# A decoder layer on one core: GpSimd sums the squares of two norms, the last output tile is multiplied ahead of its norm, and one gate operand is split in two parts

## The chip, the cores and the metric

The kernel runs on one core of one Trainium2 chip. The metric is the device time of one execution in microseconds (us), as the median of several runs. The engines are called PE (TensorE, the matrix unit), DVE (VectorE), ACT (ScalarE), POOL (GpSimd) and SP (SyncE, which here only issues transfers).

## The reference

One layer of a hybrid decoder with 1024 tokens, model width 1024 and an FFN width of 2816, all in float32. Two groups of heads (a gated delta rule and a differential attention) give `o_la` and `o_d`; what follows them is what the change touches:

```python
def rmsnorm(x, w, eps=1e-6):
    return x * lax.rsqrt(jnp.mean(x * x, axis=-1, keepdims=True) + eps) * w
...
x = x + concatenate([o_la, o_d]) @ w_out
h = rmsnorm(x, ffn_norm_w)
gate, up = split(h @ w_gate_up, 2)
x = x + (silu(gate) * up) @ w_down
return rmsnorm(x, final_norm_w)
```

## The kernel before

**Tiles and stages.** The 1024 rows are eight row tiles t = 0 to 7 of 128 rows; a row tile's 1024 columns are worked on in two halves of 512. Each float32 operand of a product is kept as two rounded parts, h (a cast on ACT) and l (a subtraction of h from the value), and a product is three matmuls, h·h, l·h and h·l. The helper `parts` (L1153) writes both: its cast runs on ACT, its subtraction on the engine given. A subtraction that helper `parts` makes bears line L1155, the cast L1154. After the attention part come four stages: the output product with the FFN norm and the transposes (about 605 to 683 us), the first block of the gate and up products, f = 0 (to 707), the loop over the remaining 21 blocks (to 1090), the down product (to 1293), and the final norm with the output (to the end at 1325.5).

**The FFN norm.** `unit_d` (L1189) runs the last matmuls of the output product for one half of one row tile; an addition on DVE (L828) puts them on the residual. Then `half_h` (L1134) squares the half on ACT with the sum of its columns as a by-product (L1140, followed by a read of the accumulator). After the second half of a tile DVE adds the two sums (L1144) and forms mean + 1e-6 (L1145), POOL raises it to the power -1/2 (L1147), and DVE multiplies both halves by this factor and the norm's weights in two `scalar_tensor_tensor` instructions (L1149). The row tiles come in the order 4, 5, 6, 7, 0, 1, 2, 3.

**The transposes.** `trans_h` (L1162) transposes a normed row tile in eight matmuls (L1166). Gate and up are computed in seven half-size products per block (Strassen's scheme in Winograd's form), so the transposed activations are quarters and sums of quarters: B11 (lower half of the width) and B21 (upper half) from the row tiles 0 to 3, B12 and B22 from 4 to 7, and T1 to T4 as sums. They carry the names hB1 (B11 and B21 together), hB22 and hT1 to hT4, with `_h` and `_l` for the parts. For t below 4 both halves of hB1 are cast in one ACT instruction 1024 wide (L1180) and subtracted in one DVE instruction 1024 wide (L1183).

**The first block.** PE runs the seven products of f = 0 in the order S3·T3, S4·B22, A11·B11, S1·T1, S2·T2, A12·B21, A22·T4 (L1381 to L1414), twelve matmuls each (L1250), and the transposes of the last row tile, `trans_h(3)`, stand between the first two in the code. The weights' sums S1 to S4 are made on DVE (L1218, L1365, L1366) and split by `parts`; `late_operands` makes those of A11, S1, S2, A12 and A22. The weights of the next block are fetched by `w_prepare`, into two buffers for the gate columns and one for the up columns, so the next up weights can only be fetched when A22 has been split.

**The end.** `final_sum` (L1566) adds the last matmuls to the residual on DVE (L1262) and squares them on ACT (L1572); `final_norm` (L1574) adds the two sums and forms the mean on DVE (L1576, L1577) and the power on POOL (L1579); `final_out` (L1582) makes the first half with a scaled copy on ACT (L1587) and a multiplication by the weights `wb3` on POOL (L1588), and the second half with one `scalar_tensor_tensor` on DVE (L1590). For the last row tile, t = 7, both halves are made on DVE. Each half is written by SP (L1592).

**What sets the order.** A scheduler orders the instructions of PE, ACT, POOL and SP, and of DVE too up to the last loop; only in the last loop (L1594 to L1603) DVE follows the order of the code:

```python
for t in range(NT):
    if t + 1 < NT: final_sum(t + 1, 0)
    ssn = final_norm(t)
    if t + 1 < NT: final_sum(t + 1, 1)
    final_out(t, ssn)
```

Each engine runs its own instructions strictly in order and waits for others by semaphores.

## Time and profile before

| | |
|---|---|
| median of 3 runs (lowest to highest) | 1322.28 us (1320.35 to 1322.42) |
| profiled execution, own time | 1327.25 us |
| profiled execution, span from first to last instruction | 1325.5 us |
| mean granted TensorE clock | 0.986 of full speed |
| PE busy | 1268.9 us, 96% of the span |
| DVE busy | 836.6 us, 63% |
| ACT busy | 537.1 us, 41% |
| POOL busy | 299.4 us, 23% |

The profiled execution is one execution; its span leaves out what lies before the first and after the last instruction, and its own time (1.75 us longer) is the figure that the runs' times compare with. Busy time of an engine says how long its instructions ran, not whether another engine waited for them; that is read from the timeline of an engine, where the idle time before an instruction stands in brackets with what ended it.

### The profile page before, as it was taken

How to read it: one execution, taken by the hardware profiler on the slowest of the kernel's cores; microseconds unless marked ns; L12 is line 12 of the kernel's file. 1: busy time of each engine (PE TensorE's matmuls, PEld its weight loads, DVE VectorE, ACT ScalarE, POOL GpSimd, SP SyncE). 2: the span in 40 equal slices, each digit the busy share in tenths (PEclk: the TensorE clock that was granted, in tenths of full speed). 3: DMA queues.
4: the chain of work that ended last, by engine and by line, in shares of the span. 5: the costliest groups of instructions: out<-in, count | busy, mean ns of one | idle time of the engine just before them, and what ended most of it. 6: DMA issues, size and time to landing. Idle time of an engine off the chain costs nothing.

```text
span 1325.5 us, 17315 instructions
## 1 busy us (share of the span) xinstructions
PE 1268.9 (96%) x6432; PEld 1064.5 (80%) x6432; DVE 836.6 (63%) x1380; ACT 537.1 (41%) x1038; POOL 299.4 (23%) x235
## 2 busy tenths in 40 slices
PE   6999989999999988999989999999999999999996
PEld 6978878898988776877768888888888888778775
DVE  6515758724766566865886655566566536687877
ACT  5324432222657555543552333333333317243314
POOL 1014443200022433023322212222212110121104
PEclk9999999989999998999989999999999999999999
DMA  7426664301053654744513343233323346666503
GB/s 222 116 64 206 219 211 136 119 17 32 17 163 118 183 192 167 208 166 176 171 47 112 112 134 108 91 119 120 112 99 108 104 159 239 206 238 207 178 13 127
DMA packets 143883, 183.43 MB, mean 138 GB/s; under 512 B 15888, under 2 KB 92984, under 8 KB 143800
## 3 DMA queue, kind: packets, MB, share of 16 engines
q1 hardware_dynamic: 135888, 168.19, 39.7%
q10 hardware_dynamic: 7912, 14.16, 2.9%
q8 instruction: 50, 0.82, 0.3%
q14 instruction: 33, 0.27, 0.1%
HBM read 127.00 MB, written 55.32 MB: 138 GB/s over the span
## 4 chain that ended last, share of the span: by engine, by line
PE 43%; DVE 5%; issue 1%; ACT 1%; DMA 1%; POOL 1%; POOLq 0%; DVEq 0%; ACTq 0%
PE big L1250 17%; PE sm L1250 8%; PE big L1549 5%; PE fl L1250 4%; PE fl L1549 3%; PE sm L1549 3%; DVE ebl L1265 1%; DMA w_raw<-in_w_gate_up 1%; DVE xh L1218 1%; PE fl L148 0%; PE fl L150 0%; PE fl L149 0%; DVE x L1262 0%; DVE av L1262 0%; DVE cv L1590 0%
## 5 line engine op out<-in xcount | busy, mean ns | idle before, releaser
L148 PE MATMUL big<-xT_h,w_h 128*128 128x512 f32 x288 | 115.6, 401 | 0.9 <-DVE ssk L500 0.5
L149 PE MATMUL big<-xT_l,w_h 128*128 128x512 f32 x288 | 113.9, 395 | 0.0
L150 PE MATMUL big<-xT_h,w_l 128*128 128x512 f32 x288 | 113.8, 396 | 0.0
L1262 DVE TENSOR_TENSOR av<-big,av 128x512 f32<-128x512 f32 x79 | 54.3, 688 | 59.5 <-PE big L1250 59.4
L161 POOL TENSOR_TENSOR w_l<-w_raw,w_h 128x512 fp32r<-128x512 f32 x32 | 42.2, 1342 | 194.8 <-ACT w_h L155 194.8
L1250 PE MATMUL big<-hT_h,cv 128*128 128x512 f32 x264 | 86.0, 390 | 0.0
L1250 PE MATMUL big<-hT_h,avl 128*128 128x512 f32 x264 | 86.0, 390 | 0.0
L148 PEld LDWEIGHTS big<-xT_h,w_h 128*128 128x128 f32 x288 | 54.6, 190 | 14.1 <-issue 2.0
L1155 POOL TENSOR_TENSOR avl<-xh,avl 128x512 fp32r<-128x512 f32 x23 | 33.2, 1444 | 138.1 <-ACT avl L1154 138.1
L150 PEld LDWEIGHTS big<-xT_h,w_l 128*128 128x128 f32 x288 | 54.4, 189 | 11.2 <-issue 0.2
L149 PEld LDWEIGHTS big<-xT_l,w_h 128*128 128x128 f32 x288 | 54.6, 190 | 10.7 <-issue 0.2
L454 POOL TENSOR_TENSOR avl<-avl 128x512 f32<-128x512 f32 x36 | 49.3, 1370 | 60.0 <-DMA avl<-in_w_down 24.8
L155 ACT CAST w_h<-w_raw 128x1024 fp32r<-128x1024 f32 x32 | 33.4, 1052 | 67.6 <-PE big L149 32.2
L1155 POOL TENSOR_TENSOR cv<-xh,cv 128x512 fp32r<-128x512 f32 x22 | 30.8, 1400 | 132.5 <-ACT cv L1154 132.5
L1250 PE MATMUL sm<-hB_h,avl 128*128 128x512 f32 x176 | 58.8, 396 | 1.1 <-ACT hB_h L1180 1.1
L1250 PEld LDWEIGHTS big<-hT_h,avl 128*128 128x128 f32 x264 | 49.6, 188 | 10.4 <-DVE av L1262 0.2
L1527 POOL TENSOR_TENSOR x<-x,w_raw 128x512 f32<-128x512 f32 x16 | 22.9, 1438 | 154.4 <-DVE x L1262 122.7
L1250 PE MATMUL sm<-hB_h,cv 128*128 128x512 f32 x176 | 57.8, 389 | 0.0
L1250 PEld LDWEIGHTS big<-hT_h,cv 128*128 128x128 f32 x264 | 49.6, 188 | 10.2
L992 ACT ACTIVATE ae<-big,mx 128x128 f32<-128x128 f32 (+7 forms) x64 | 47.1, 739 | 23.7 <-DVE mx L983 15.7
L157 DVE TENSOR_TENSOR w_l<-w_raw,w_h 128x1024 fp32r<-128x1024 f32 x16 | 21.6, 1347 | 51.1 <-ACT w_h L155 35.0
L1218 DVE TENSOR_TENSOR xh<-w_raw 128x512 f32<-128x512 f32 x45 | 31.5, 701 | 33.7 <-DMA w_raw<-in_w_gate_up 33.7
(455 smaller groups left out, 3708.2 us busy)
## 6 DMA issues: line engine op xcount, KB each, us to landing
w_raw<-in_w_gate_up SPq DMA_DIRECT2D x44, 512.0 KB, 4.0
w_raw<-in_w_in SPq DMA_DIRECT2D x24, 512.0 KB, 5.6
sum<-av SPq DMA_DIRECT2D x45, 256.0 KB, 3.1
avl<-in_w_down SPq DMA_DIRECT2D x18, 512.0 KB, 5.3
rows<-avl SPq DMA_DIRECT2D x18, 512.0 KB, 3.0
w_raw<-sum SPq DMA_DIRECT2D x11, 512.0 KB, 3.6
xh<-sum SPq DMA_DIRECT2D x21, 256.0 KB, 3.8
av<-sum SPq DMA_DIRECT2D x10, 512.0 KB, 4.3
```

Of the source, the lines that this page charges most:

```text
L148: nc.tensor.matmul(ps, lhsT=lh, rhs=rh, start=start, stop=False)
L149: nc.tensor.matmul(ps, lhsT=lh, rhs=rl, start=False, stop=False)
L150: nc.tensor.matmul(ps, lhsT=ll, rhs=rh, start=False, stop=stop)
L155: nc.scalar.copy(out=h, in_=raw)
L161: eng.tensor_tensor(out=l[:, c], in0=raw[:, c], in1=h[:, c].bitcast(F32), op=ALU.subtract)
L454: nc.gpsimd.tensor_tensor(out=o, in0=x, in1=y, op=ALU.subtract)
L992: nc.scalar.activation(out=e[:, :n].rearrange("p (b c) -> p b c", b=nb), in_=s[:, :, :w], func=AF.Exp, bias=mx[:, m:m + 1], accum_out=zs[: ...
L1155: eng.tensor_tensor(out=l, in0=raw, in1=h.bitcast(F32), op=ALU.subtract)
L1218: nc.vector.tensor_tensor(out=r, in0=a0, in1=a1, op=alu)
L1250: nc.tensor.matmul(ps, lhsT=x[:, k, :], rhs=y[:, k, :], start=begin and k == 0 and n == 0, stop=k == HALF - 1 and n == 2, skip_group_check ...
L1262: nc.vector.tensor_tensor(out=out, in0=in0, in1=in1, op=ALU.add)
L1549: nc.tensor.matmul(pss[i], lhsT=x[:, g_, ts], rhs=y[:, g_, :], start=begin and g_ == 0 and n_ == 0, stop=g_ == GRP - 1 and n_ == 2, skip_g ...
```

## The change

Three edits.

1. A new helper `mean_power` takes the place of the two DVE instructions and the POOL power in both norms. POOL adds the two sums and 1e-6 in one `tensor_scalar` and then raises to the power. The factor 1/D moves into ACT's squaring, as a scale of D^-0.5 on its input. This is done eight times in `half_h` and eight times in `final_norm`; 32 DVE instructions on 128x1 go, 16 POOL instructions on 128x1 come.
2. In the last loop the product of row tile 7's first half with `wb3` is computed on POOL before its norm's factor is known; ACT then scales it in place by the factor. Row tile 6 has both halves made by DVE, without ACT and POOL.
3. In `trans_h(3)` alone, B11's two parts are made by an ACT cast and a DVE subtraction 512 wide ahead of T1 and T2, and B21's parts by another such pair behind them.

```diff
+    def mean_power(ss):
+        nc.gpsimd.tensor_scalar(out=ss[:, 0:1], in0=ss[:, 0:1], scalar1=ss[:, 1:2], scalar2=1e-6, op0=ALU.add, op1=ALU.add)
+        nc.gpsimd.tensor_tensor(out=ss[:, 1:2], in0=ss[:, 0:1], in1=epow_neg[:, 0:1], op=ALU.pow)
...
-        nc.scalar.activation(out=xns[t][:, us], in_=x2t[t][:, us], func=AF.Square, accum_out=sss[t][:, u:u + 1])
+        nc.scalar.activation(out=xns[t][:, us], in_=x2t[t][:, us], func=AF.Square, scale=D ** -0.5,
+                             accum_out=sss[t][:, u:u + 1])
...
-        nc.vector.tensor_tensor(out=ss[:, 0:1], in0=ss[:, 0:1], in1=ss[:, 1:2], op=ALU.add)
-        nc.vector.tensor_scalar(out=ss[:, 0:1], in0=ss[:, 0:1], scalar1=1.0 / D, scalar2=1e-6,
-                                op0=ALU.mult, op1=ALU.add)
-        nc.gpsimd.tensor_tensor(out=ss[:, 1:2], in0=ss[:, 0:1], in1=epow_neg[:, 0:1], op=ALU.pow)
+        mean_power(ss)
...
-        nc.scalar.copy(out=first[0][:, :, cs], in_=ptv)
+        if t == 3:
+            parts(B11[0][:, :, cs], B11[1][:, :, cs], lo, nc.vector)
+        else:
+            nc.scalar.copy(out=first[0][:, :, cs], in_=ptv)
         nc.vector.tensor_tensor(out=f1, in0=f1, in1=lo, op=ALU.subtract)
         nc.vector.tensor_tensor(out=f2, in0=lo, in1=f2, op=ALU.add)
-        nc.vector.tensor_tensor(out=first[1][:, :, cs], in0=ptv, in1=first[0][:, :, cs].bitcast(F32), op=ALU.subtract)
+        if t == 3:
+            parts(B21[0][:, :, cs], B21[1][:, :, cs], hi, nc.vector)
+        else:
+            nc.vector.tensor_tensor(out=first[1][:, :, cs], in0=ptv, in1=first[0][:, :, cs].bitcast(F32),
+                                    op=ALU.subtract)
...
     def final_out(t, ssn):
-        o = cvt()
+        o = late.pop("o") if t == NT - 1 else cvt()
         for n in range(2):
             ns = slice(n * 512, (n + 1) * 512)
-            if n == 0 and t < NT - 1:
+            if n == 1 or t == NT - 2:
+                nc.vector.scalar_tensor_tensor(out=o[:, ns], in0=x2[:, t, ns], scalar=ssn[:, 1:2],
+                                               in1=wb3[:, ns], op0=ALU.mult, op1=ALU.mult)
+            elif t == NT - 1:
+                nc.scalar.activation(out=o[:, ns], in_=o[:, ns], func=AF.Copy, scale=ssn[:, 1:2])
+            else:
                 nc.scalar.activation(out=o[:, ns], in_=x2[:, t, ns], func=AF.Copy, scale=ssn[:, 1:2])
                 nc.gpsimd.tensor_tensor(out=o[:, ns], in0=o[:, ns], in1=wb3[:, ns], op=ALU.mult)
...
+            if t + 1 == NT - 1:
+                late["o"] = cvt()
+                nc.gpsimd.tensor_tensor(out=late["o"][:, n0], in0=x2[:, t + 1, n0], in1=wb3[:, n0], op=ALU.mult)
             ssn = final_norm(t)
```

The scheduler gives other orders for the changed code, also where the code reads the same. Rows of the changed kernel bear its own lines: L1152 there is L1149 before, L1157 and L1158 are L1154 and L1155, L1228 is L1218. In the rows a name's number tells instances of a buffer apart.

**DVE around the sums of row tiles 6 and 7**, about 624 to 636 us. L828 on avl_5525 makes row tile 6 (from PE's results fl), on avl_5559 row tile 7; L1149 with ssh_5701, ssh_5711 and ssh_5737 is the product with the weights of row tiles 5, 6 and 7; hB22_l and cv are parts of `trans_h(4)`. Before:

```order
L1144 TENSOR_TENSOR ssh_5701<-ssh_5701 128x1
L1145 TENSOR_SCALAR ssh_5701<-ssh_5701 128x1
L1149 SCALAR_TENSOR_TENSOR w_raw_5700<-avl_5519,ssh_5701,wb2_4572 128x512
L828 TENSOR_TENSOR avl_5525<-fl_5610,avl_5525 128x512
L1149 SCALAR_TENSOR_TENSOR w_raw_5700<-avl_5519,ssh_5701,wb2_4572 128x512
L828 TENSOR_TENSOR avl_5525<-fl_5624,avl_5525 128x512
...
L1149 SCALAR_TENSOR_TENSOR avl_5736<-avl_5559,ssh_5737,wb2_4572 128x512
L1155 TENSOR_TENSOR hB22_l_5681<-big_5720,hB22_h_5680 128x4x128
L1175 TENSOR_TENSOR cv_5729<-big_5720,cv_5729 128x512
```

and now:

```order
L1152 SCALAR_TENSOR_TENSOR w_raw_5699<-avl_5519,ssh_5700,wb2_4572 128x512 x2
L828 TENSOR_TENSOR avl_5525<-fl_5610,avl_5525 128x512
L828 TENSOR_TENSOR avl_5525<-fl_5624,avl_5525 128x512
...
L1152 SCALAR_TENSOR_TENSOR avl_5733<-avl_5559,ssh_5734,wb2_4572 128x512 x2
L1158 TENSOR_TENSOR hB22_l_5681<-big_5717,hB22_h_5680 128x4x128
L1178 TENSOR_TENSOR cv_5726<-big_5717,cv_5726 128x512
```

The pairs of L1144 and L1145 are gone, and the two products of one norm now stand together, the second ahead of the next L828 (or ahead of `trans_h(4)`'s subtractions) instead of behind it.

**ACT and POOL around the product A11·B11**, about 665 to 683 us. On ACT, hB1_h is the cast of `trans_h(3)`, sm is PE's result of A11·B11, copied to av (L1392 before, L1402 now), hT4_h is a part of T4, and avl from xh_6088 (before) or xh_6082 (now) is S1's h part. Before:

```order
L1180 CAST hB1_h_5678<-big_6051 128x8x128
L1154 CAST hT1_h_5682<-cv_5833 128x4x128
L1154 CAST hT2_h_5684<-cv_5833 128x4x128
L1154 CAST hT4_h_5688<-xh_6060 128x4x128
L1154 CAST avl_6092<-xh_6088 128x512
L1154 CAST avl_6101<-w_raw_5801 128x512
L1392 COPY av_6036<-sm_6033 128x512
```

and now:

```order
L1157 CAST hB1_h_5678<-big_6043 128x4x128
L1157 CAST hT1_h_5682<-cv_5828 128x4x128
L1157 CAST hB1_h_5678<-big_6043 128x4x128
L1157 CAST hT2_h_5684<-cv_5828 128x4x128
L1402 COPY av_6028<-sm_6025 128x512
L1157 CAST hT4_h_5688<-xh_6052 128x4x128
L1157 CAST avl_6086<-xh_6082 128x512
L1157 CAST avl_6095<-w_raw_5797 128x512
```

hB1_h is two casts; the copy of A11·B11's result, which waits for PE's last matmul of that product, now stands ahead of T4's and S1's h parts. On POOL, cv from xh_5967 (before) or xh_5960 (now) is S4's l part, ssh_5989 or ssh_5982 the sums of row tile 3, and avl_6092 or avl_6086 S1's l part. Before:

```order
L1155 TENSOR_TENSOR cv_5971<-xh_5967,cv_5971 128x512
L1155 TENSOR_TENSOR hT1_l_5683<-cv_5792,hT1_h_5682 128x4x128
L1147 TENSOR_TENSOR ssh_5989<-ssh_5989,expo_134 128x1
L1155 TENSOR_TENSOR hT1_l_5683<-cv_5833,hT1_h_5682 128x4x128
L1155 TENSOR_TENSOR avl_6092<-xh_6088,avl_6092 128x512
```

and now:

```order
L1136 TENSOR_SCALAR ssh_5982<-ssh_5982 128x1
L1137 TENSOR_TENSOR ssh_5982<-ssh_5982,expo_134 128x1
L1158 TENSOR_TENSOR cv_5964<-xh_5960,cv_5964 128x512
L1158 TENSOR_TENSOR hT1_l_5683<-cv_5788,hT1_h_5682 128x4x128
L1158 TENSOR_TENSOR hT1_l_5683<-cv_5828,hT1_h_5682 128x4x128
L1158 TENSOR_TENSOR avl_6086<-xh_6082,avl_6086 128x512
```

Row tile 3's sum and power have moved ahead of S4's l part.

**POOL in the last loop**, the three last row tiles. The multiplications by the weights are L1588 before and L1602 now, the powers L1579 and L1137. Before:

```order
L1579 TENSOR_TENSOR ssn_10774<-ssn_10774,expo_134 128x1
L1588 TENSOR_TENSOR cv_10826<-cv_10826,wb2_9137 128x512
L1579 TENSOR_TENSOR ssn_10803<-ssn_10803,expo_134 128x1
L1588 TENSOR_TENSOR cv_10855<-cv_10855,wb2_9137 128x512
L1579 TENSOR_TENSOR ssn_10832<-ssn_10832,expo_134 128x1
```

and now:

```order
L1602 TENSOR_TENSOR cv_10814<-cv_10814,wb2_9131 128x512
L1136 TENSOR_SCALAR ssn_10792<-ssn_10792 128x1
L1137 TENSOR_TENSOR ssn_10792<-ssn_10792,expo_134 128x1
L1613 TENSOR_TENSOR cv_10831<-x2_9137,wb2_9131 128x512
L1136 TENSOR_SCALAR ssn_10820<-ssn_10820 128x1
L1137 TENSOR_TENSOR ssn_10820<-ssn_10820,expo_134 128x1
```

The sum stands between the multiplication of the row tile before and the power; row tile 7's own product (L1613) has taken the place of row tile 6's multiplication, and waits neither for row tile 6's norm nor for ACT.

## Rows read from the trace of the kernel before

**Rows 1.** Busy time by engine in three stretches, granted PE clock, DMA.

```profile
core 0: us, PE busy (x) PEld busy (x) DVE busy (x) ACT busy (x) POOL busy (x), PEclk, DMA share, GB/s
...
660.00:668.00 8.00, 4.80 (x23) 3.56 (x24) 7.99 (x14) 5.17 (x10) 1.57 (x2) 0.95 0.17 68
668.00:682.00 14.00, 10.94 (x32) 8.28 (x33) 10.80 (x16) 5.16 (x9) 4.36 (x4) 0.66 0.00 0
...
707.00:1090.00 383.00, 383.00 (x1690) 317.33 (x1691) 218.35 (x337) 120.87 (x201) 81.84 (x60) 1.00 0.36 115
```

**Rows 2.** Timeline of PE: start, us, operation, idle before and its releaser.

```profile
625.56 0.50 PE L148 MATMUL fl<-w_h,cv 128*128 128x512 f32 x1 [0.21 <-DVE avl L828]
...
667.77 1.22 PE L1250 MATMUL big<-hB_h,cv 128*128 128x512 f32 x2 [0.64 <-POOL cv L1155]
...
677.67 0.80 PE L1250 MATMUL sm<-hB_l,avl 128*128 128x512 f32 x1 [1.95 <-DVE hB_l L1183]
...
682.20 0.62 PE L1250 MATMUL big<-hT_h,avl 128*128 128x512 f32 x2
...
706.94 0.50 PE L1250 MATMUL big<-hB_h,avl 128*128 128x512 f32 x1 [0.45 <-DVE av L1262]
```

**Rows 3.** Timeline of DVE, 623 to 625 us: row tile 5's product and row tile 6.

```profile
624.15 0.75 DVE L1149 SCALAR_TENSOR_TENSOR w_raw<-avl,ssh,wb 128x512 f32<-128x512 f32 x1 [0.73 <-POOL ssh L1147]
624.82 0.68 DVE L828 TENSOR_TENSOR avl<-fl,avl 128x512 f32<-128x512 f32 x1
```

**Rows 4.** Timelines of ACT and DVE, 648 us: one whole norm.

```profile
648.14 0.19 ACT L1140 ACTIVATION_READ_ACCUMULATOR avl<-avl 128x1 f32 x1
...
648.36 0.16 DVE L1144 TENSOR_TENSOR ssh<-ssh 128x1 f32<-128x1 f32 x1 [0.93 <-ACT avl L1140]
...
649.46 1.42 DVE L1149 SCALAR_TENSOR_TENSOR avl<-avl,ssh,wb 128x512 f32<-128x512 f32 x2 [0.76 <-POOL ssh L1147]
```

**Rows 5.** Timelines of ACT, POOL and DVE, 665 to 683 us.

```profile
665.60 0.19 ACT L1140 ACTIVATION_READ_ACCUMULATOR avl<-avl 128x1 f32 x1
...
666.43 1.29 POOL L1155 TENSOR_TENSOR cv<-xh,cv 128x512 fp32r<-128x512 f32 x1 [6.46 <-ACT cv L1154]
...
674.15 1.01 ACT L1180 CAST hB_h<-big 128x1024 fp32r<-128x1024 f32 x1 [0.60 <-PE big L1166]
...
680.62 1.71 DVE L1155 TENSOR_TENSOR avl<-w_raw,avl 128x512 fp32r<-128x512 f32 x1
```

**Rows 6.** The chain that ended last: the piece at 682 us.

```profile
682.35 4.02 DMA w_raw<-in_w_gate_up
```

**Rows 7.** Busy time by engine while A11·B11 ran, columns of Rows 1.

```profile
677.50:680.50 3.00, 2.83 (x7) 2.25 (x8) 3.00 (x6) 1.68 (x3) 0.74 (x2) 0.50 0.00 0
```

**Rows 8.** Timelines of DVE and POOL in the last loop.

```profile
1298.24 0.15 DVE L1576 TENSOR_TENSOR ssn<-ssn 128x1 f32<-128x1 f32 x1
...
1309.88 0.75 DVE L1576 TENSOR_TENSOR ssn<-ssn 128x1 f32<-128x1 f32 x1
...
1320.67 1.41 DVE L1590 SCALAR_TENSOR_TENSOR cv<-x,ssn,wb 128x512 f32<-128x512 f32 x2 [0.75 <-POOL ssn L1579]
...
1309.32 1.30 POOL L1588 TENSOR_TENSOR cv<-cv,wb 128x512 f32<-128x512 f32 x1 [0.84 <-ACT cv L1587]
1310.99 0.55 POOL L1579 TENSOR_TENSOR ssn<-ssn,expo 128x1 f32<-128x1 f32 x1 [0.38 <-DVE ssn L1577]
...
1317.07 0.55 POOL L1579 TENSOR_TENSOR ssn<-ssn,expo 128x1 f32<-128x1 f32 x1 [0.38 <-DVE ssn L1577]
```

**Rows 9.** Groups of POOL by shape: busy us, mean ns, idle before.

```profile
L1046 POOL TENSOR_TENSOR ams<-ams,expo 128x4 f32<-128x4 f32 x8 | 8.1, 1007 | 53.8 <-DVE ams L1045 28.1 <-DMA aql<-ql 25.7
...
L1147 POOL TENSOR_TENSOR ssh<-ssh,expo 128x1 f32<-128x1 f32 x8 | 4.4, 553 | 14.7 <-DVE ssh L1145 9.2 <-ACT cv L1173 5.2 <-ACT hB_h L1154 0.4
...
L1627 POOL MEMSET const-float32-1.0<- 128x1 f32 x1 | 0.1, 98 | 0.0
```

**Rows 10.** Line L1592, SP's output transfers: duration ns min/median/max, first and last start.

```profile
L1592 SPq DMA_DIRECT2D out<-cv x16: 332/336/391, 1301.5 to 1322.1; - x16
```

More of the change, by code (lines that the diff above doesn't have):

```diff
@@ L1571, in final_sum @@
         add(x2[:, t, ns], plain(t, n, (NF - 2, NF - 1)), x2[:, t, ns])
-        nc.scalar.activation(out=sc[:, ns], in_=x2[:, t, ns], func=AF.Square, accum_out=ssn[:, n:n + 1])
+        nc.scalar.activation(out=sc[:, ns], in_=x2[:, t, ns], func=AF.Square, scale=D ** -0.5, accum_out=ssn[:, n:n + 1])
     def final_norm(t):
         ssn = sq.pop(t)[0]
-        nc.vector.tensor_tensor(out=ssn[:, 0:1], in0=ssn[:, 0:1], in1=ssn[:, 1:2], op=ALU.add)
-        nc.vector.tensor_scalar(out=ssn[:, 0:1], in0=ssn[:, 0:1], scalar1=1.0 / D, scalar2=1e-6,
-                                op0=ALU.mult, op1=ALU.add)
-        nc.gpsimd.tensor_tensor(out=ssn[:, 1:2], in0=ssn[:, 0:1], in1=epow_neg[:, 0:1], op=ALU.pow)
+        mean_power(ssn)
         return ssn
     def final_out(t, ssn):
-        o = cvt()
+        o = late.pop("o") if t == NT - 1 else cvt()
         for n in range(2):
             ns = slice(n * 512, (n + 1) * 512)
-            if n == 0 and t < NT - 1:
+            if n == 1 or t == NT - 2:
[4 more added lines that the diff above has]
+            else:
                 nc.scalar.activation(out=o[:, ns], in_=x2[:, t, ns], func=AF.Copy, scale=ssn[:, 1:2])
                 nc.gpsimd.tensor_tensor(out=o[:, ns], in0=o[:, ns], in1=wb3[:, ns], op=ALU.mult)
-            else:
-                nc.vector.scalar_tensor_tensor(out=o[:, ns], in0=x2[:, t, ns], scalar=ssn[:, 1:2],
-                                               in1=wb3[:, ns], op0=ALU.mult, op1=ALU.mult)
             nc.sync.dma_start(out=out[0, t * P:(t + 1) * P, ns], in_=o[:, ns])
```

## Prediction

> **What bounds the kernel now.** I read the windows by stage first. PE is the bound almost everywhere: in the loop from 707 to 1090 us it is busy 383.00 of 383.00, so what reaches 707 late ends late. It has gaps where norm, transposes and the first block meet: from 660 to 682 it is busy 4.80 + 10.94 of 22 us, at a granted clock of 0.95 and 0.66 [rows 1]. That leaves 6.3 us of idle time there, and what half the clock adds to the matmuls. The other place is the end, where PE has run out of work and ACT, DVE and POOL pass a row tile from one to the other. The timeline of PE then tells who is waited for: DVE's L828 at 625.56, POOL's l part of S4 at 667.77, DVE's 1024-wide subtraction of hB1 at 677.67 (1.95 us, the longest), and DVE again at 706.94 [rows 2]. The chain that ended last passes through the fetch of the next up weights at 682.35 [rows 6], which goes on to the wait at 706.94.
>
> The sum below is made against the profiled execution, 1327.25 us (span 1325.5), which is 4.97 above the median of the runs, 1322.28. I put the difference that it gives on the median. About 0.2%, 2.64 us, is what a measurement of this kernel can tell from no change.
>
> **The price of POOL's sum, a.** No row of before has a POOL `tensor_scalar` of this form. The nearest rows are a memset of 128x1, which reads nothing, at 0.10 us, and the power of 128x1 at 0.55 [rows 9]. The power of 128x4 takes 1.01, so a column of it costs 0.15 and 0.40 is fixed. I take a = 0.25, halfway between 0.10 and 0.40, and keep 0.10 and 0.55 as ends. The power now waits for POOL's own result; I take 0.1 for that hand-off.
>
> **One FFN norm.** Before, from the end of the accumulator's read (648.33) to the product with the weights (649.46) went 1.13 us [rows 4]. Now it is 0.1 + 0.25 + 0.1 + 0.55 + 0.03 = 1.03, that is -0.1 (from -0.25 to +0.2). By itself it is next to nothing, since PE has work of other row tiles under most norms. The two DVE instructions removed, 0.15 each, are covered too, except that DVE is busy 7.99 of 8 us from 660 to 668 [rows 1].
>
> **The order ahead of 667 us.** The second product of a norm now stands ahead of the next L828. There it costs 0.67 (from 624.15 to 624.82 one such product and the step to the next instruction [rows 3]), and PE had waited for that L828 with 0.21 idle [rows 2], so nothing covers it: about +0.5 for PE. The same comes once more for row tile 7 ahead of the subtractions of `trans_h(4)`. Together I take +1.1; the bounds are 0, if PE's queued matmuls take it up, and 2 x 0.67 = 1.34. Then POOL's sum and power of row tile 3 stand ahead of S4's l part, which the third matmul of S4·B22 waited for at 667.77 [rows 2]. The read of the squares ended at 665.79 and S4's l part began at 666.43 [rows 5]. Now it begins 0.1 + 0.25 + 0.1 + 0.55 behind the read, at 666.8: +0.35, and +0.75 more if DVE's product, released by the same power, goes first. I take +0.5, bounds 0 and 1.1. So the transposes of row tile 3 end 1.6 later, at 675.75 (bounds 0 and 2.4).
>
> **The split of hB1.** From the start of the 1024-wide cast at 674.15 [rows 5] to PE's second matmul of A11·B11 at 677.67 [rows 2] went 3.52 us. Now ACT casts 512 columns (an estimate of 0.62 from the 1.01 for 1024) and DVE subtracts 512 (0.68, as L828 does [rows 3]); with hand-offs this is 1.35, so A11·B11 goes on 2.2 earlier against its transposes. What is late next is S1. Its h part stands on ACT behind the copy of A11·B11's result and T4's h part, and POOL's l part behind that. Counted from the end of the transposes: at full clock (0.23 us a matmul) the product's remaining eleven end at 1.35 + 2.5 = 3.9; DVE has seven instructions of 0.6 to 0.7 ahead of S1's sum and one wait for ACT, so S1's h part is ready at about 6.2, its l part 1.3 to 1.6 later, at 7.7. Before, S1·T1's third matmul, the first to use that l part, came at 682.20 - 674.15 = 8.05 [rows 2, 5]. The gain of 2.2 thus shrinks to 0.3: the wait moves from inside A11·B11 to the start of S1·T1. The fetch of the next up weights waits for DVE's split of A22, which before ran 1.71, from 680.62 [rows 5], and released the transfer 8.2 after the transposes [rows 6]. Now it comes behind POOL's S1 at about 8.4: +0.2. With the shift of 1.6 this gives PE +1.3 at S1·T1 and +1.8 at the fetch. The chain through it had 0.45 us of idle PE at its end [rows 2], so it does set the start at 707. I take +1.7 for the stage (bounds -1.0 and +3.5).
>
> **The last loop.** Before, L1576 took 0.15 us while POOL was idle and 0.75 while POOL multiplied, ending with the multiplication's end: 1309.88 + 0.75 = 1310.63, against 1309.32 + 1.30 = 1310.62 [rows 8]. From there to the power at 1310.99 went 0.37. Now POOL's sum follows its own multiplication, then the power: a + 0.1 = 0.35. So taking the addition off DVE frees nothing here, since POOL's sum is queued behind the same multiplication. Per row tile -0.02, five times -0.1; with a = 0.10 -0.85, with a = 0.55 +1.4.
>
> For row tile 7 before, 4.46 us went from the end of row tile 6's power (1317.07 + 0.55) to the end of the last product (1320.67 + 1.41 = 1322.08) [rows 8]. Now POOL starts row tile 7's product there (1.30), while DVE wants row tile 6's two halves (1.41). The rows of L1576 show such a pair one after the other. If POOL's product, sum and power come first, 1.30 + 0.25 + 0.1 + 0.55 = 2.2, and the last halves (0.75) end at 1320.6: -1.45. If both halves go ahead of the sum, they end at 1322.0: -0.05. I take -0.7. Against it stands SP: both last halves are now ready together, and SP takes 0.34 to 0.39 to issue each [rows 10], so the last one goes out 0.35 later: net -0.35 (bounds -1.1 and +0.3). The loop together: -0.45 (bounds -1.95 and +1.7).
>
> The Trainium skill (SBUF — State Buffer, Who interferes with whom) says that a VectorE instruction with two SBUF inputs and a GpSimd instruction that reads SBUF exclude each other for a whole instruction. The 0.75 of L1576 agrees; by a reading in which they only slow each other a little, this term would be -1.1.
>
> **Sum.** +1.7 - 0.45 = +1.25, so 1322.28 + 1.25 = 1323.5 us.
>
> **The rivals.**
>
> *Slower: half the clock carries over.* While A11·B11 ran, PE was granted 0.50, 1.2 GHz, after its idle time before 677.67 [rows 2, 7]. Before, that cost little, since S1 was no sooner ready. Now ACT's copy of that product stands ahead of S1's h part, so if the clock is at 0.50 again, eleven matmuls at 0.43 instead of 0.23 put S1, and the fetch behind it, off by 2.2: 1323.5 + 2.2 = 1325.7. It decides when the granted clock is low for most of A11·B11. For it: PE waits here twice still. Against it: the wait is shorter, about 0.7 (cast to second matmul 1.35 in place of 3.52) against 1.95.
>
> *Hidden order.* PE's queued matmuls take up what DVE and POOL are late ahead of 667, so the 1.6 falls away. Then the stage is at about 0.1, with the last loop -0.35: 1321.9. Against it stand the waits at 625.56 and 667.77 [rows 2], which have no slack.
>
> *Faster.* The sum costs 0.10, the last row tile's product gets ahead of DVE, the shift falls away and S1 is ready 1.2 sooner, because DVE's queue runs without gaps: -1.2 - 1.95 = -3.15, so 1319.1. For it: DVE was held 1.0 of its 1.71 at 680.62 by POOL [rows 5], which could fall otherwise now.
>
> *GpSimd is dear.* The sum costs as much as the power, 0.55: the loop's five row tiles give +1.5 more than forecast, the last one and the FFN norm of row tile 3 +0.3 each: 1325.6. The memset's 0.10 [rows 9] speaks against so much for one column without a power. The Trainium skill (GPSIMD Engine Reference, Engine selection) advises VectorE for elementwise work, with GpSimd about twice as slow for two inputs; DVE's 0.15 doubled would be 0.30, which bears out the middle value rather than this one.
>
> That the change does nothing, since POOL stood behind its multiplication before as well, gives 1322.3 and lies within the hidden order.
>
> **How the numbers follow.** Forecast 0.40, half the clock 0.17, hidden order 0.25, faster 0.12, GpSimd dear 0.06. Below 1319.64 (faster) lie most of the faster case, 0.10, and the low end of the hidden order, 0.03: 0.13. Above 1324.92 (slower) lie 0.14 of the clock's case, 0.05 of the dear one and 0.03 of the forecast's upper end: 0.22. The rest is 0.65. The range that leaves out 2 in 10 runs from 1319.2, near the faster case, to 1326.4, past the clock's.
>
> **What would show it.** A POOL sum of 0.15 to 0.35; PE's second matmul of A11·B11 1.2 to 1.5 behind its first cast; a new wait of about 1 us or more ahead of the first matmuls of S1·T1, put down to ACT or POOL; the matmul at 706.94 some 1.7 later; the powers in the last loop still about 3.04 apart (1310.99 to 1317.07 are two row tiles [rows 8]); the last two halves ending together, some 0.7 earlier. I am wrong if S1·T1 starts without a wait, if the transposes of row tile 3 are not late, or if the powers come 2.8 or 3.4 apart.

## The result and the profile after

| | before | after |
|---|---|---|
| median of 21 runs each, side by side (lowest to highest) | 1321.68 us (1317.69 to 1332.65) | 1328.53 us (1322.55 to 1334.30) |
| ratio, 95% interval | | 1.0054 (1.0040 to 1.0068) |
| profiled execution, own time | 1327.25 us | 1325.84 us |
| its span, mean granted clock | 1325.5 us, 0.986 | 1324.1 us, 0.988 |

The change makes the kernel slower by 0.54%, 7.1 us on 1322 (5.3 to 9.0). The forecast was 1323.5, the range ended at 1326.4. The two profiled executions stand the other way round. So the first thing to do is to find out from where the two can be compared at all. PE's waits in the output product give the place: the first wait shown below lies ahead of all changed code, and between it and the second lies one changed norm only, that of row tile 4. Timeline of PE, before, rows that were not shown above:

```profile
611.98 0.50 PE L148 MATMUL fl<-w_h,cv 128*128 128x512 f32 x1 [0.47 <-DVE avl L828]
622.34 0.50 PE L148 MATMUL fl<-w_h,cv 128*128 128x512 f32 x1 [1.65 <-DVE avl L828]
636.46 1.06 PE L1166 MATMUL big<-ident,w_raw 128*128 128x128 f32 x8 [0.21 <-DVE cv L1175]
672.21 1.91 PE L1166 MATMUL big<-ident,avl 128*128 128x128 f32 x8
681.74 0.39 PE L1250 MATMUL big<-hT_h,avl 128*128 128x512 f32 x1
```

and after:

```profile
606.17 0.50 PE L148 MATMUL fl<-w_h,cv 128*128 128x512 f32 x1 [0.28 <-DVE avl L828]
616.64 0.50 PE L148 MATMUL fl<-w_h,cv 128*128 128x512 f32 x1 [1.77 <-DVE avl L828]
620.50 0.50 PE L148 MATMUL fl<-w_h,cv 128*128 128x512 f32 x1 [0.84 <-DVE avl L828]
632.02 1.06 PE L1169 MATMUL big<-ident,w_raw 128*128 128x128 f32 x8 [0.82 <-DVE cv L1178]
665.56 0.73 PE L1260 MATMUL big<-hB_h,cv 128*128 128x512 f32 x2 [0.51 <-POOL cv L1158]
670.22 1.06 PE L1169 MATMUL big<-ident,avl 128*128 128x128 f32 x8 [2.11 <-DVE xh L1194]
672.69 0.80 PE L1260 MATMUL sm<-hB_l,avl 128*128 128x512 f32 x1
679.46 0.51 PE L1260 MATMUL big<-hT_h,avl 128*128 128x512 f32 x1 [1.71 <-ACT avl L1157]
680.82 0.73 PE L1260 MATMUL big<-hT_h,avl 128*128 128x512 f32 x2 [0.62 <-POOL avl L1158]
707.41 0.50 PE L1260 MATMUL big<-hB_h,avl 128*128 128x512 f32 x1 [0.64 <-DVE av L1272]
```

The first of these rows stands 5.81 us earlier after than before, the second 5.70, so that row tile 4's norm costs 0.11. The 5.81 lie ahead of the change, in code that is the same in both, and most of them are the clock's. Two windows of that part, before, with the columns of [rows 1]:

```profile
260.00:280.00 20.00, 20.00 (x131) 18.72 (x130) 10.62 (x13) 6.84 (x10) 2.50 (x2) 0.78 0.11 29
280.00:300.00 20.00, 20.00 (x218) 19.02 (x217) 5.22 (x10) 3.25 (x7) 0.00 (x0) 0.96 0.01 2
```

and the first of them after:

```profile
260.00:280.00 20.00, 20.00 (x182) 18.86 (x181) 10.90 (x16) 7.22 (x11) 2.51 (x2) 1.00 0.11 28
```

PE is busy all the time in both, but before it was granted 0.78 and 0.96, which by an estimate from these rows is (0.22 + 0.04) x 20 = 5.2 us. Five of the fourteen profiles of this case (before, E1, E5, E8 and E9) show such a stretch there, and nothing in their code sets them apart. The whole span hides the change behind it. From the second wait on (622.34 and 616.64, called the mark below) the two can be laid side by side. The table gives the distance from the mark, worked out from the rows above and [rows 2].

| PE reaches | before | after | later |
|---|---|---|---|
| first output product behind row tile 6's L828 | 3.22 | 3.86 | 0.64 |
| transposes of row tile 6 | 14.12 | 15.38 | 1.26 |
| third matmul of S4·B22 (needs S4's l part) | 45.43 | 48.92 | 3.49 |
| transposes of row tile 3 | 49.87 | 53.58 | 3.71 |
| second matmul of A11·B11 | 55.33 | 56.05 | 0.72 |
| first matmul of S1·T1 | 59.40 | 62.82 | 3.42 |
| third matmul of S1·T1 | 59.86 | 64.18 | 4.32 |
| first matmul of the loop | 84.60 | 90.77 | 6.17 |

So the norm's part costs 3.7, the split gives 3.0 of it back, and the start of S1·T1 with what follows costs 5.45. The column "before" is one execution too, and behind the mark its clock was low: its transposes of row tile 3 took 1.91 us against 1.06. Two kernels of the experiments, E3 and E4, have the code of before up to the last loop. In their timelines of PE the loop starts at these places, first E3, then E4:

```profile
702.53 0.50 PE L1255 MATMUL big<-hB_h,avl 128*128 128x512 f32 x1 [0.70 <-DVE av L1267]
...
700.91 0.50 PE L1255 MATMUL big<-hB_h,avl 128*128 128x512 f32 x1 [0.32 <-DVE av L1267]
```

That is 83.69 and 83.10 from their marks (618.84 and 617.81), where before needed 84.60. Against them the loop of the change starts 7.1 to 7.7 later, and the runs say 7.1.

What delays the norm's part stands in the timelines of DVE and POOL. DVE, before:

```profile
657.98 1.22 DVE L1183 TENSOR_TENSOR hB_l<-big,hB_h 128x1024 fp32r<-128x1024 f32 x1
660.01 1.42 DVE L1149 SCALAR_TENSOR_TENSOR avl<-avl,ssh,wb 128x512 f32<-128x512 f32 x2
664.35 0.69 DVE L828 TENSOR_TENSOR avl<-sm,avl 128x512 f32<-128x512 f32 x1
666.87 1.22 DVE L1183 TENSOR_TENSOR hB_l<-big,hB_h 128x1024 fp32r<-128x1024 f32 x1
669.49 1.42 DVE L1149 SCALAR_TENSOR_TENSOR avl<-avl,ssh,wb 128x512 f32<-128x512 f32 x2 [1.40 <-POOL ssh L1147]
670.82 0.69 DVE L1184 TENSOR_TENSOR xh<-big,cv 128x512 f32<-128x512 f32 x1
```

DVE and then POOL, after:

```profile
654.72 2.40 DVE L1152 SCALAR_TENSOR_TENSOR avl<-avl,ssh,wb 128x512 f32<-128x512 f32 x2 [0.66 <-POOL ssh L1137]
657.05 1.21 DVE L1192 TENSOR_TENSOR hB_l<-big,hB_h 128x1024 fp32r<-128x1024 f32 x1
661.78 0.68 DVE L828 TENSOR_TENSOR avl<-sm,avl 128x512 f32<-128x512 f32 x1
664.30 3.45 DVE L1152 SCALAR_TENSOR_TENSOR avl<-avl,ssh,wb 128x512 f32<-128x512 f32 x2 [0.64 <-POOL ssh L1137]
668.27 1.21 DVE L1192 TENSOR_TENSOR hB_l<-big,hB_h 128x1024 fp32r<-128x1024 f32 x1
669.40 0.68 DVE L1194 TENSOR_TENSOR xh<-big,cv 128x512 f32<-128x512 f32 x1
...
654.66 1.26 POOL L1158 TENSOR_TENSOR hT_l<-cv,hT_h 128x512 fp32r<-128x512 f32 x1
663.32 0.30 POOL L1136 TENSOR_SCALAR ssh<-ssh 128x1 f32<-128x1 f32 x1 [7.40 <-ACT avl L1145]
663.70 0.56 POOL L1137 TENSOR_TENSOR ssh<-ssh,expo 128x1 f32<-128x1 f32 x1
664.23 1.27 POOL L1158 TENSOR_TENSOR cv<-xh,cv 128x512 fp32r<-128x512 f32 x1
665.46 1.74 POOL L1158 TENSOR_TENSOR hT_l<-cv,hT_h 128x512 fp32r<-128x512 f32 x1
```

The sum takes 0.30 us, near the 0.25 taken. But the pair of products with the weights takes 2.40 us for row tile 2 and 3.45 for row tile 3, where before both took 1.42. Each time a POOL subtraction starts within 0.07 us of the pair. For row tile 3 there are two of them, S4's l part and T1's, and the second takes 1.74 instead of 1.3: they take turns. DVE loses 1.0 + 2.0 us to this collision.

The new order on DVE costs nearly as much. Before, the last subtractions of `trans_h` (L1183 for hB1's l part, now L1192, and its neighbours) stood ahead of the pair; now two of them stand behind it, at row tile 2 and again at row tile 3. From the start of row tile 2's pair to row tile 3's second addition (L828) went 4.34 us before and go 7.06 after (660.01 to 664.35, 654.72 to 661.78): 0.98 of the difference is the collision, 1.74 the order. Row tile 3's squares are read 3.1 later by that. Its pair starts only 0.5 later from the mark, since its power no longer stands behind POOL's two subtractions as before (the wait of 1.40 at 669.49). From the pair's start to the end of L1184, now L1194, went 2.02 and go 5.78: 2.03 of it is the collision, 1.73 the order. PE then waits 2.11 for L1194, DVE's last use of the transposes before (at 670.22).

The windows over A11·B11 and S1·T1, after, with the columns of [rows 1]:

```profile
672.00:677.50 5.50, 5.50 (x12) 3.76 (x12) 4.32 (x7) 1.70 (x3) 1.29 (x1) 0.50 0.00 0
677.50:680.80 3.30, 0.99 (x3) 0.30 (x2) 1.88 (x2) 2.66 (x5) 1.28 (x1) 0.90 0.00 0
680.80:684.60 3.80, 3.78 (x10) 3.01 (x11) 2.92 (x5) 1.14 (x2) 0.00 (x0) 0.60 0.33 96
```

A11·B11 runs at 0.50, as before [rows 7], then PE idles 2.3 us, and S1·T1 runs at 0.60 where before it ran at full clock.

In the last loop, the timelines of POOL and DVE, after:

```profile
1312.94 0.56 POOL L1137 TENSOR_TENSOR ssn<-ssn,expo 128x1 f32<-128x1 f32 x1
...
1316.08 0.56 POOL L1137 TENSOR_TENSOR ssn<-ssn,expo 128x1 f32<-128x1 f32 x1
1316.61 1.26 POOL L1613 TENSOR_TENSOR cv<-x,wb 128x512 f32<-128x512 f32 x1
1317.97 0.62 POOL L1136 TENSOR_SCALAR ssn<-ssn 128x1 f32<-128x1 f32 x1
1318.67 0.84 POOL L1137 TENSOR_TENSOR ssn<-ssn,expo 128x1 f32<-128x1 f32 x1
...
1316.68 2.41 DVE L1596 SCALAR_TENSOR_TENSOR cv<-x,ssn,wb 128x512 f32<-128x512 f32 x2 [1.20 <-POOL ssn L1137]
1319.54 0.75 DVE L1596 SCALAR_TENSOR_TENSOR cv<-x,ssn,wb 128x512 f32<-128x512 f32 x1 [0.45 <-POOL ssn L1137]
```

From row tile 6's power to the last product's end is 3.65 us (1316.64 to 1320.29) against 4.46 [rows 8], 0.81 less; the end of the span comes 3.81 behind that, against 3.42 before (1325.5 - 1322.08), 0.39 more; a row tile takes 3.14 to 3.18 against 3.04. Here too the pair of products takes 2.41 beside POOL's product, and even the sum and the power are stretched, to 0.62 and 0.84. From PE's last matmul to the end of the span go 10.62 before and 10.95 after, 0.3 more: the loop is worth little either way.

### The profile page after: what moved, and what is told of

Same layout as the page of the kernel before. It is cut to its first block, busy times and chain, and to the rows that moved or that the text cites. A ratio compares the mean times of both kernels' runs of the same rounds, so it can differ in the third digit from the quotient of the medians.

```text
span 1324.1 us, 17306 instructions
## 1 busy us (share of the span) xinstructions
PE 1266.6 (96%) x6432; PEld 1059.9 (80%) x6432; DVE 831.1 (63%) x1349; ACT 537.3 (41%) x1039; POOL 302.9 (23%) x251
## 4 chain that ended last, share of the span: by engine, by line
PE 44%; DVE 3%; issue 2%; POOL 1%; ACT 1%; DMA 0%; POOLq 0%; DVEq 0%; ACTq 0%
PE big L1260 17%; PE sm L1260 8%; PE big L1559 5%; PE fl L1260 4%; PE fl L1559 3%; PE sm L1559 3%; DVE ebl L1275 0%; DMA w_raw<-in_w_gate_up 0%; DVE av L1272 0%; DVE xh L1228 0%; PE fl L150 0%; PE fl L149 0%; PE fl L148 0%; DVE x L1272 0%; PE sm L149 0%
## 5 line engine op out<-in xcount | busy, mean ns | idle before, releaser
L1158 POOL TENSOR_TENSOR avl<-xh,avl 128x512 fp32r<-128x512 f32 x23 | 31.8, 1382 | 143.1 <-ACT avl L1157 143.1
L1158 POOL TENSOR_TENSOR cv<-xh,cv 128x512 fp32r<-128x512 f32 x22 | 30.8, 1400 | 125.8 <-ACT cv L1157 125.8
L1228 DVE TENSOR_TENSOR xh<-w_raw 128x512 f32<-128x512 f32 x45 | 31.2, 694 | 33.9 <-DMA w_raw<-in_w_gate_up 33.9
L1260 PE MATMUL big<-hT_l,cv 128*128 128x512 f32 x132 | 52.3, 396 | 0.0
```

The costliest lines, as they stand in the source:

```text
L1158: eng.tensor_tensor(out=l, in0=raw, in1=h.bitcast(F32), op=ALU.subtract)
L1228: nc.vector.tensor_tensor(out=r, in0=a0, in1=a1, op=alu)
L1260: nc.tensor.matmul(ps, lhsT=x[:, k, :], rhs=y[:, k, :], start=begin and k == 0 and n == 0, stop=k == HALF - 1 and n == 2, skip_group_check ...
```

## The experiments

Theory and rival were set up in two rounds. In the first: the loss comes from GpSimd's sums in the FFN norm (theory 1), or from the split, which puts S1 behind the copy of A11·B11's result (theory 2). Four parts of the change were timed one at a time. All ratios are to runs of the kernel before on the same chip (twelve runs of each kernel, six of E1, and 29 to 35 of the kernel before), with their 95% interval; "distance" is PE's distance from the mark, as in the table above.

**E1, GpSimd's sums in the FFN norm alone.**

```diff
-        nc.scalar.activation(..., func=AF.Square, accum_out=sss[t][:, u:u + 1])
+        nc.scalar.activation(..., func=AF.Square, scale=D ** -0.5, accum_out=sss[t][:, u:u + 1])
...
-        nc.vector.tensor_tensor(out=ss[:, 0:1], ...)
-        nc.vector.tensor_scalar(out=ss[:, 0:1], ...)
-        nc.gpsimd.tensor_tensor(out=ss[:, 1:2], ..., op=ALU.pow)
+        mean_power(ss)
```

> Only the FFN norm's sums go to GpSimd; the last loop and trans_h(3) stay as before. Theory 1 (the loss is made by this edit: the two products of a norm stand together on DVE, and GpSimd's S4 part comes behind the sum and the power and shares a port with DVE's products): 3 to 6 us slower than before, and the transposes of row tile 3 come 3 to 4 us later against the first output-product wait near 612. Theory 2 (the loss is made by the split of hB1, which puts S1 behind the copy of A11*B11): within 1.5 us of before.

Measured: 1.0064 (1.0044 to 1.0083). The transposes of row tile 3 lie at 53.57 from the mark, as in the whole change (53.58); the loop starts at 88.72, 4.12 later than before. This part alone makes a loss as large as the whole change's, 8.5 us (5.8 to 11.0), more than the 3 to 6 expected. Its pairs of products, timeline of DVE:

```profile
661.95 2.40 DVE L1151 SCALAR_TENSOR_TENSOR avl<-avl,ssh,wb 128x512 f32<-128x512 f32 x2 [0.66 <-POOL ssh L1136]
671.52 3.45 DVE L1151 SCALAR_TENSOR_TENSOR avl<-avl,ssh,wb 128x512 f32<-128x512 f32 x2 [0.64 <-POOL ssh L1136]
```

**E2, the split of hB1 alone.**

```diff
+        if t == 3:
+            parts(B11[0][:, :, cs], B11[1][:, :, cs], lo, nc.vector)
...
+        if t == 3:
+            parts(B21[0][:, :, cs], B21[1][:, :, cs], hi, nc.vector)
```

> Only hB1 of row tile 3 is split; all norms as before. Theory 1: between 2 us faster and 1.5 us slower, since PE's second matmul of A11*B11 comes about 2 us earlier and most of it is given back at the start of S1*T1. Theory 2: 3 to 6 us slower, with A11*B11 and S1*T1 at half the clock.

Measured: 1.0016 (0.9999 to 1.0033), between the two theories' numbers and nearer theory 1. PE's second matmul of A11·B11 is at 51.80 from the mark, 3.5 earlier than before; 1.3 of that is the low clock of the profile before, and against E4, with the same code up to there, it is 2.2 earlier, as the prediction had it. The loop starts at 85.42, 0.8 later than before and 1.7 to 2.3 later than in E3 and E4. What eats the gain stands in the timeline of PE and in the windows over A11·B11, the wait and S1·T1:

```profile
674.40 0.66 PE L1257 MATMUL big<-hT_h,avl 128*128 128x512 f32 x1 [2.15 <-ACT avl L1154]
...
676.09 1.22 PE L1257 MATMUL big<-hT_h,avl 128*128 128x512 f32 x2 [0.60 <-POOL avl L1155]
```

```profile
668.60:672.20 3.60, 3.29 (x12) 2.17 (x12) 2.88 (x5) 1.74 (x4) 1.30 (x1) 1.00 0.00 0
672.20:676.00 3.80, 1.13 (x3) 0.37 (x2) 3.80 (x6) 3.38 (x7) 1.58 (x1) 0.81 0.00 0
676.00:680.90 4.90, 4.82 (x11) 3.80 (x12) 2.79 (x5) 0.43 (x1) 0.03 (x1) 0.50 0.50 145
```

A11·B11 is at full clock, PE then idles 2.15 for S1's h part and 0.60 for its l part, and S1·T1 comes at 0.50. So the split alone may cost some 2 us; by the runs that cannot be told from nothing.

**E3, the last loop alone; E4, only row tile 7's product ahead**, sums of both norms on DVE. E4's diff against E3:

```diff
-        mean_power(ssn)
+        nc.vector.tensor_tensor(out=ssn[:, 0:1], in0=ssn[:, 0:1], in1=ssn[:, 1:2], op=ALU.add)
+        nc.vector.tensor_scalar(out=ssn[:, 0:1], in0=ssn[:, 0:1], scalar1=1.0 / D, scalar2=1e-6, ...)
+        nc.gpsimd.tensor_tensor(out=ssn[:, 1:2], in0=ssn[:, 0:1], in1=epow_neg[:, 0:1], op=ALU.pow)
```

> Only the last loop is changed (GpSimd's sums and row tile 7's product ahead). Both theories: within 1 us of before: five row tiles each 0.12 longer (+0.6), the last row tile 0.8 shorter, the last transfer issued 0.4 behind the end. If it is over 1.5 us slower, the last loop has a share of the loss that the profiles do not show.

> Only row tile 7's product comes ahead and row tile 6 goes to DVE; the sums of both norms stay on DVE. Both theories: 0.3 to 1.2 us faster than before, and about 0.6 faster than the run with GpSimd's sums in the last loop; powers again 3.05 us apart.

Measured: E3 1.0002 (0.9987 to 1.0018), E4 1.0006 (0.9991 to 1.0021). Neither can be told from before. E4's expected gain did not show: there DVE makes row tile 6's two halves ahead of row tile 7's sum, which stands behind them in DVE's order. The last loop has no share in the loss that the runs can tell.

The larger part of the loss is thus E1's. The second round asks why. Theory A: GpSimd's sum is the cause, because it puts S4's l part off and lets POOL's subtractions and DVE's products block each other. Theory B: any shorter chain of the norm would do it, because the scheduler then puts the two products together ahead of the next addition.

**E5, the sum as one DVE instruction.** The order on DVE changes only in part as in E1: row tile 3's pair moves ahead of `trans_h`'s subtraction for hB1's l part, row tile 2's stays behind it.

```diff
-        nc.gpsimd.tensor_scalar(out=ss[:, 0:1], in0=ss[:, 0:1], scalar1=ss[:, 1:2], ...)
+        nc.vector.tensor_scalar(out=ss[:, 0:1], in0=ss[:, 0:1], scalar1=ss[:, 1:2], ...)
```

> The FFN norm's sum is one DVE instruction in place of GpSimd's (the squares scaled on ACT as in the change); last loop and hB1 as before. Theory A (GpSimd's sum is the loss: it puts GpSimd's S4 part off and lets GpSimd's subtractions block DVE's two products of a norm): within 2 us of before, the products of row tile 3 at most 2.4 us. Theory B (any shorter chain of the norm lets the scheduler put the two products together ahead of the next addition, and that order is the loss): 4 to 8 us slower than before, as with GpSimd's sum.

Measured: 1.0018 (0.9999 to 1.0037), +2.4 us. The loop starts at 86.06 from the mark, 1.46 later than before. Row tile 2's pair takes 1.41, row tile 3's 2.44, since only T1's subtraction is beside it. That speaks for theory A, though it is a little over the 2 us expected: by theory B the loss would be 4 to 8 us. It does not rule out that the order has a share, since one of the two pairs keeps its old place.

**E6, only row tile 3's sum on DVE, the others on POOL.**

```diff
+        if t in (3,):
+            nc.vector.tensor_scalar(out=ss[:, 0:1], in0=ss[:, 0:1], scalar1=ss[:, 1:2], ...)
+            nc.gpsimd.tensor_tensor(out=ss[:, 1:2], ..., op=ALU.pow)
+        else:
+            mean_power(ss)
```

> GpSimd makes the FFN norm's sums except for row tile 3, whose sum is one DVE instruction, so that S4's part comes ahead of the power again on GpSimd. Theory A: 2 to 4 us faster than with all sums on GpSimd, the third matmul of S4*B22 1 us or more earlier against the output-product wait near 622 (48.9 us behind it with all sums on GpSimd, 45.4 before). Theory B: as slow as with all sums on GpSimd.

Measured: 1.0025 (1.0005 to 1.0046), 5 us less than E1 by the ratios, more than the 2 to 4 expected. But the third matmul of S4·B22 lies at 48.56 from the mark, only 0.3 earlier than in E1, against the 1 us expected, and the loop starts 1.1 earlier. So the time went the way of theory A, and by more than the profile of one execution explains; row tile 3's pair takes 2.44 in place of 3.45.

**E7, no subtraction of POOL beside the products.** POOL keeps all eight sums.

```diff
-        parts(T1[0][:, :, cs], T1[1][:, :, cs], f1, nc.gpsimd)
+        parts(T1[0][:, :, cs], T1[1][:, :, cs], f1, nc.vector if t in (1, 2) else nc.gpsimd)
...
-    W0["S4"] = w_split(s4, nc.gpsimd)
+    W0["S4"] = w_split(s4, nc.vector)
```

> GpSimd makes the FFN norm's sums, but S4's l part and T1's l parts of row tiles 1 and 2 are made on DVE, so that GpSimd has no subtraction beside the products of row tiles 2 and 3; DVE gets three more instructions of 0.6 us. Theory A: the products take 1.42 us a pair again (2.40 and 3.45 with the collision), and the kernel is 1 to 4 us faster than with all sums on GpSimd, in spite of DVE's 1.8 us more. Theory B: as slow or slower, by up to 2 us.

Measured: 1.0021 (0.9998 to 1.0045). Timeline of DVE:

```profile
657.49 1.42 DVE L1151 SCALAR_TENSOR_TENSOR avl<-avl,ssh,wb 128x512 f32<-128x512 f32 x2 [0.66 <-POOL ssh L1136]
667.77 1.42 DVE L1151 SCALAR_TENSOR_TENSOR avl<-avl,ssh,wb 128x512 f32<-128x512 f32 x2 [0.53 <-POOL ssh L1136]
```

Both pairs take 1.42 again, the transposes of row tile 3 lie at 51.68, 1.9 earlier than in E1, the loop starts 2.1 earlier (86.58), and by the ratios the kernel is 0.43% faster than E1, 5.7 us where 1 to 4 were expected, though DVE does 1.8 us more. The pairs still stand ahead of the subtractions, as in E1.

**E9, the same moves in the kernel before**, as a control (the two lines of E7's diff, sums as before).

> The kernel before, with S4's l part and T1's l parts of row tiles 1 and 2 made on DVE: the control for the run without the collision. Before, the products of row tiles 2 and 3 took 1.42 us a pair already, so there is no collision to take away. If the gain of the run without the collision came from the collision: 0 to 3 us slower than before (DVE has 1.8 us more). If it came from S4's part being faster on DVE whatever the norm does: 2 to 4 us faster than before.

Measured: 1.0007 (0.9987 to 1.0026). Where there is no collision, the moves gain nothing. **E12, the same moves in the whole change:**

> The whole change, with S4's l part and T1's l parts of row tiles 1 and 2 made on DVE. If the collision and S4's place behind the sum are the largest part of the loss: 3 to 6 us faster than the change, 1 to 4 us slower than before. If the split with its order and clock holds it: as slow as the change.

Measured: 1.0021 (1.0001 to 1.0042), against the change's 1.0054: 4.4 us of its 7.1 are gone (1324.49 us median against 1328.53), as an estimate from the two intervals between 1 and 8 us. Both expected ranges are met.

What is left of the loss is about 0.2% in E5, E6, E7 and E12 alike. By E9 it is not the moved subtractions. It fits the order on DVE, the additions that come later (0.64 at the first place of the table) and, in E12, the split's own loss; no run separates these.

**E8 and E10, the split with S1 first.** Both make S1's sum ahead of the transposes of row tile 3, so that its h part no longer stands behind the copy of A11·B11's result; E8 on POOL, E10 on DVE. The diff is E10's, without the lines that it takes out of `late_operands`; E8 has `nc.gpsimd` for the sum.

```diff
     product(pc, W0["S3"], T3, True)
+    W0["A11"] = w_split(a11, nc.vector)
+    late["s1"] = scratch()
+    nc.vector.tensor_tensor(out=late["s1"], in0=a21, in1=a22, op=ALU.add)
+    W0["S1"] = w_split(late["s1"], nc.gpsimd)
     trans_h(3)
```

> The split of hB1 alone, with S1's sum made on GpSimd and split ahead of the transposes of row tile 3, so that S1 no longer stands behind the copy of A11*B11's result. If the split's gain is eaten by the wait for S1 and the clock that falls in it: no wait of over 0.7 us at S1*T1, S1*T1 at full clock, 1 to 4 us faster than before. If the fetch of the next up weights or DVE's queue sets the start of the loop anyway: within 1 us of before.

> The split of hB1 with S1's sum on DVE ahead of hB1's l part, so that S1 stands ahead of the copy of A11*B11's result and GpSimd has nothing beside row tile 3's products. If clock and S1 were what ate the split's gain: no wait of over 0.7 us at S1*T1, all products from A11*B11 on at full clock, 1 to 3 us faster than before. If not: within 1 us of before.

Measured: E8 1.0003 (0.9982 to 1.0025), E10 0.9996 (0.9977 to 1.0015). In E8 the wait at S1·T1 is gone, but POOL's sum, put beside row tile 3's pair, stretches it to 2.42, PE waits 2.32 ahead of the transposes, and A11·B11 is at half the clock: the collision again. In E10 no collision is left. Windows over its A11·B11 and S1·T1:

```profile
671.50:675.30 3.80, 3.12 (x13) 2.35 (x13) 3.80 (x6) 3.18 (x6) 2.29 (x2) 1.00 0.00 0
675.30:678.40 3.10, 2.98 (x13) 2.18 (x12) 3.10 (x5) 1.21 (x2) 0.44 (x1) 1.00 0.58 169
```

Both products are at full clock, as expected, and yet the time stays that of before: further on PE waits 0.88 us for DVE (L1269). That DVE's queue takes back what the split had freed is not shown; in E11's profile, with the same code there, this wait is 0.17, and two of the products run at about 0.6 of the clock.

**E11, E10 with row tile 7's product ahead** (E4's edit).

> The same with row tile 7's product ahead (all sums of norms on DVE): the candidate that should beat both kernels. 1 to 4 us faster than before if the run with the split and S1 first is faster by 1 to 3; otherwise within 1 us of before.

Measured: 0.9979 (0.9958 to 1.0000), 1318.57 us median against 1321.16. By the ratios it is 0.7% faster than the change, and it may beat the kernel before, but the interval ends at 1: this is not settled. Its gain of 2.8 us fits neither expectation well, since E10 was not faster.

**All runs against the mark.** The start of the loop from the mark, how much later that is than in E3 and E4, and the loss by the runs:

| | loop starts | later than E3, E4 | by the runs (95% interval) |
|---|---|---|---|
| before | 84.60 | 0.9 to 1.5 | |
| the change | 90.77 | 7.1 to 7.7 | 7.1 (5.3 to 9.0) |
| E1, the sums in the FFN norm | 88.72 | 5.0 to 5.6 | 8.5 (5.8 to 11.0) |
| E2, the split | 85.42 | 1.7 to 2.3 | 2.1 (-0.1 to 4.4) |
| E5, sum on DVE | 86.06 | 2.4 to 3.0 | 2.4 (-0.1 to 4.9) |
| E6, row tile 3's sum on DVE | 87.65 | 4.0 to 4.6 | 3.3 (0.7 to 6.1) |
| E7, E1 without collision | 86.58 | 2.9 to 3.5 | 2.8 (-0.3 to 5.9) |
| E12, the change without collision | 89.07 | 5.4 to 6.0 | 2.8 (0.1 to 5.5) |

By the mark E1 and E2 together make 6.7 to 7.9, about the whole change. The collision is worth some 2 us by the mark (E1 less E7, the change less E12) and 4.4 to 5.7 by the runs. So it is shown to be a part of the loss; that it is the largest part is not shown. Where the runs and the profiles differ, the clock is one reason. The mean granted clock over the runs was 0.9874 for the change and 0.9863 for E1, against 0.990 to 0.991 for before; E7 and E12 had 0.9897 and 0.9901. Among before's own runs 0.001 of it goes with about 1 us, so by an estimate some 3 us of the change's 7 and 4 of E1's 8.5 go with the lower clock. Whether the waits of these kernels lower it, or the stretch between 260 and 300 us by chance, is not shown.

## Why the prediction was wrong

- **The price of the sum** was right: 0.30 against 0.25 taken. So the rival "GpSimd is dear" was not it: the sum by itself stayed below the power (0.56), and the last loop alone (E3) cost nothing that the runs can tell.
- **The second product ahead of the next addition** was right in size: 1.26 us later at row tile 6's transposes against +1.1.
- **"The order ahead of 667 us" is the step that failed**: its second half, which made row tile 3's transposes 1.6 later (bounds 0 and 2.4). They came 3.7 later, 4.2 against E4. The 0.35 for S4's place was right: its l part began 0.64 behind the squares' read before and 1.01 in E1. Two things were mis-sized. The collision was allowed for once, with 0.75 for one product and 0.5 for all; the pairs of row tiles 2 and 3 lost 1.0 and 2.0, because they now start with POOL's subtractions rather than after them. And DVE's new order was counted at row tiles 6 and 7 only, for want of a row from the others; at row tiles 2 and 3 it cost 1.74 and 1.73 more. 2.6 came back, since row tile 3's power no longer waits behind two subtractions. The path was another one too: the forecast carried the lateness through S4's l part, but the transposes waited for DVE's L1194. E7 took the collision away: the transposes came 1.9 earlier than in E1, and the runs were 0.43% faster. For the order there is no such experiment.
- **The split** was right at its own place: 1.37 us from the cast's start at 671.32 to the second matmul (672.69), 1.35 forecast. The forecast that S1 would eat the gain was right too, but its size was not: S1·T1's third matmul came 9.5 behind the end of the transposes, 7.7 forecast.
- **Half the clock**, given 0.17 as a rival, did come: eleven matmuls of A11·B11 at 0.43, the copy behind them, S1 behind the copy. But E2 shows that it comes at S1·T1 even where A11·B11 was at full clock, and the clock of one product differs between executions of the same code (last section). The rival put the time at 1325.7; in this execution the low clock came on top of the collision, not in its place.
- **The last loop**: -0.81 + 0.39 and five times about 0.12, together +0.2, or +0.3 from PE's last matmul on, against -0.45 forecast. The missed piece is 0.1 us between POOL's multiplication and its sum, which the prediction took as nothing. Its two parts for row tile 7, -0.7 and +0.35, came out at -0.81 and +0.39.
- **The range** ended at 1326.4 because the bounds of the collision were set from one product. The Trainium skill (SBUF — State Buffer, Who interferes with whom), which was used for the last loop, calls the port pair that the two engines share an exclusive lock. The 2.40 and 3.45 agree: DVE lost 0.98 beside a POOL subtraction of 1.26, and 2.03 beside two of 1.27 and 1.74. The prediction weighed this where a POOL product stood beside two DVE products; in the FFN norm it did so for one product only, where three POOL subtractions stood beside four.
- **The rivals** stand as argued, but for a slip: "hidden order" at 1321.9 goes with the last loop at -0.45, and with the -0.35 named there it is 1322.0.

## What to carry to other kernels

When a small instruction is moved to GpSimd to shorten a chain, look at what the chain releases: if it releases a VectorE instruction with two inputs in SBUF, and GpSimd has its own two-input work queued behind the small one, both start at once and, in these traces, hold each other up. Price every such pair that starts together, not one of them. A shorter chain also moves its consumers ahead in another engine's order: price what they now stand in front of, at every tile. A gain in front of a wait is worth what the next late operand leaves of it.

Two profiles of different kernels are compared from a common mark near the change. Here the whole spans said 1.4 us faster where the runs said 7 us slower, and a low clock in unchanged code made most of the difference. One profile of the kernel before is not enough either: two kernels that are unchanged up to the place differed from it by 0.9 to 1.5 us.

## What the runs showed of the hardware

- A GpSimd `tensor_scalar` on 128x1 takes 0.30 us, 0.62 beside DVE products; the power of 128x1 takes 0.56 and 0.84 there.
- A pair of DVE products of 128x512 takes 1.42 us alone, 2.40 beside one GpSimd subtraction and 3.45 beside two.
- Behind the waits of this stage PE was granted 0.50 for a whole product in some executions (A11·B11 before and in the change, S1·T1 in E2), with 0.43 us for a matmul in place of 0.23. The same code behind the same waits was also granted full clock: S4·B22 ran at 0.59 in E3 and at 1.00 in E4, A11·B11 at 1.00 in E3 and 0.61 in E4, and at 1.00 in E10 and 0.60 in E11. What decides it is not shown.
